# Two of a pair's four weight sums by a ScalarE copy and an accumulating DMA, their tile in the residual's slots

## The chip, the core and the metric

The kernel runs on one core of a Trainium2 chip. TensorE (PE, with its weight loads as PEld), VectorE (DVE), ScalarE (ACT), GpSimd (POOL) and SyncE (SP) each work through their own list of instructions in order; an instruction that waits for a semaphore holds back all that stand behind it on its engine. DMAs are issued here by SP and POOL (a few by ACT) and land later. The metric is the device time of one execution in microseconds.

## What is computed

One layer of a decoder trunk over 512 tokens of width 2048, all in f32: a gated linear attention (GLA) mixer, a squared-ReLU MLP, a gated projection of a per-layer embedding, and a final norm:

```python
u = rmsnorm(h, norm_mix[i])
h = h + gla_mixer(u, ...)                                            # projections, chunked scan, w_out
h = h + jnp.square(jax.nn.relu(rmsnorm(h, norm_mlp[i]) @ w_up[i])) @ w_down[i]   # 2048 -> 8192 -> 2048
gate = jax.nn.sigmoid(rmsnorm(h, norm_ple[i]) @ w_ple_gate[i])
h = h + gate * (p[i] @ w_ple_proj[i])
return rmsnorm(h, norm_final)
```

The change lies in the product with `w_up` alone.

## The kernel before

Activations lie transposed, features on the partitions and the 512 tokens in the free dimension. An f32 product is made of three matmuls on float32r operands: each operand is split into `hi` (a cast by ScalarE) and `lo` (value minus `hi`, by VectorE), and hi·hi, hi·lo and lo·hi are summed in PSUM.

**The MLP** takes most of the time. `up_group(g)`, g = 0 to 31, makes 256 of the 8192 hidden features. The product with `w_up` is done by the Strassen-Winograd scheme: of each pair of 128-row blocks (`kp`, 0 to 7) and the two 128-column halves, seven products on blocks of 128x128 by 128x256 take the place of eight. Beside the raw weight blocks B11, B12, B21, B22 it needs four sums of weights, T1 to T4. One step `k4` (0 to 3) of an up group covers two values of `kp`:

- SP loads `raw_up`, 128x4x256 (512 KB), into one of the 3 `raw` buffers, which it shares in turn with `raw_dn`.
- VectorE forms the sums in the tile `T` (128x2x4x128): at L780 two of them at once (B12 and B21, each plus B11), at L782 and L783 the other two, each from the one before.
- for each `kp` ScalarE casts the three raw blocks and the four sums into `whi_up` (L790, two instructions), VectorE subtracts into `wlo_up` (L791, two), and PE runs 21 matmuls (L797 to L799). `whi` and `wlo` have 4 buffers each, in turn for up and down.

After its four steps the up group's products are combined (tile `e`, by ScalarE L803 and VectorE L804 to L811), squared and split into `Sh` and `Sl` (L813 to L817).

`down_group(c, g)` adds 512 hidden features (two up groups) times `w_down` into 256 of the 2048 outputs: POOL loads the residual tile `h` from `h_d` in DRAM (L845), SP loads `raw_dn`, ScalarE and VectorE split it (`whi_dn` L130, `wlo_dn` L132), PE runs 24 matmuls, VectorE adds the product onto `h` (L854, two instructions, called the evacuation below), and POOL stores `h` to `h_d` (L860). In the last round (c = 15) `h` stays on chip in another tile.

The loop over `c` interleaves them. One up group with its share of down groups is called **a half** below: up steps 0 and 1, down, up step 2, down, up step 3, down, the combination, down. So a half has four T tiles, T_0 to T_3, and four h tiles, h_0 to h_3, in the order T_0, T_1, h_0, T_2, h_1, T_3, h_2, h_3. The two up groups of c = 0 have no down groups beside them; after the last up group eight down groups follow.

The buffers: `T` has one buffer of its own (`sum`); `h` takes one of the three buffers of the tag `ld` (`load`), which before the MLP hold the residual `xres` of the output projection. `sums` also gives the differences `D` of the activations before the MLP and the squares after it.

The order of each engine's list and the buffers that the tiles get are set when the program is built, by a scheduler that takes the instructions by the place where the code writes them and by a buffer becoming free; on the chip the lists are fixed, and semaphores let them wait for each other.

Of the kernel before, what the change touches and what calls it, by code (L numbers as in the profile page):

```python
# [9 lines left out]
F32 = mybir.dt.float32  # L10
# [4 lines left out]
ALU = mybir.AluOpType  # L15

P = 128
# [42 lines left out]
def trunk_kernel(ctx, tc, a, out):  # L60
    nc = tc.nc

    const = ctx.enter_context(tc.tile_pool(name="const", bufs=1))
    wpool = ctx.enter_context(tc.tile_pool(name="wpool", bufs=4))
# [9 lines left out]
    def slot(shape, name, dtype=F32):  # L74
        return spool.tile(shape, dtype, tag="s", name=name)
# [4 lines left out]
    def bank(name):  # L80
        return mm.tile([P, 512], F32, tag="mm", name=name)
# [53 lines left out]
    def w_rows(w, k0, nk, c0, nc_):  # L135
        return w[k0 * P:(k0 + nk) * P, c0:c0 + nc_].rearrange("(k p) c -> p k c", p=P)
# [89 lines left out]
    X = [None] * NK  # L226

    def load(shape, name):
        return wpool.tile(shape, F32, tag="ld", name=name, bufs=3)

    xc = [None] * (NK // 2)

    def x_load(cc):
        xc[cc] = load([P, NTT, 256], f"x_{cc}")
        nc.sync.dma_start(xc[cc], x2[:, cc * 256:(cc + 1) * 256].rearrange("(j p) c -> p j c", p=P))
# [69 lines left out]
    for k in range(NK):  # L305
# [6 lines left out]
        if k == 0:  # L312
# [5 lines left out]
            for b in range(2):  # L318
                t = slot([P, NK // 2, P], f"lr_w{b}", F32R)
# [264 lines left out]
    def load_gated(i):  # L584
        raw = load([P, T], f"gr_{i}")
        nc.gpsimd.dma_start(raw, gated_d[i])
        split_gated(i, raw)
# [68 lines left out]
    tpool = mlp.enter_context(tc.tile_pool(name="tpool", bufs=1))  # L656
# [8 lines left out]
    def wide(name):  # L665
        return tpool.tile([P, 8, HT], F32, tag="w", name=name)

    def sums(name):
        return tpool.tile([P, 2, 4, P], F32, tag="sum", name=name)

    acc2 = const.tile([P, T], F32, name="acc2")

# [31 lines left out]
    def operands(kp, u):  # L704

        a_, runs = operand_slots(kp)
        ub = u.rearrange("p k (h t) -> p (k h) t", h=2)
        d = sums(f"D_{kp}").rearrange("p a b c -> p (a b c)").rearrange("p (o t) -> p o t", t=HT)
        nc.vector.tensor_tensor(out=d[:, 0, :], in0=ub[:, 1, :], in1=ub[:, 3, :], op=ALU.subtract)
        nc.vector.tensor_tensor(out=d[:, 1, :], in0=ub[:, 0, :], in1=ub[:, 1, :], op=ALU.subtract)  # L710
        nc.vector.tensor_tensor(out=d[:, 2, :], in0=ub[:, 0, :], in1=d[:, 0, :], op=ALU.subtract)
        nc.vector.tensor_tensor(out=d[:, 3, :], in0=ub[:, 2, :], in1=d[:, 2, :], op=ALU.subtract)
        for n_run in range(len(runs[0])):
            o, n, hi = runs[0][n_run]
            lo = runs[1][n_run][2]
            for q_ in range(n):
                blk = (0, 2, 3)[o + q_]
                if q_ and (0, 2, 3)[o + q_ - 1] == blk - 1:
                    continue
                m = 2 if q_ + 1 < n and (0, 2, 3)[o + q_ + 1] == blk + 1 else 1  # L720
                src = ub[:, blk:blk + m, :]
                nc.scalar.copy(hi[:, q_:q_ + m, :], src)
                nc.vector.tensor_tensor(
                    out=lo[:, q_:q_ + m, :], in0=src, in1=hi[:, q_:q_ + m, :].bitcast(F32), op=ALU.subtract)
        nc.scalar.copy(a_[0], d)
        nc.vector.tensor_tensor(out=a_[1], in0=d, in1=a_[0].bitcast(F32), op=ALU.subtract)
# [4 lines left out]
    def evac_out(i, ps):  # L731
        kp = i // 2
        if i % 2 == 0:
            late["x"] = load([P, 2, T], f"xres_{kp}")
            nc.gpsimd.dma_start(late["x"], xT_d[i:i + 2].rearrange("k p t -> p k t"))
            if kp in (5, 6):
                late["u"] = extra([P, 2, T], f"u_{kp}")
            else:
                late["u"] = wide(f"u_{kp}").rearrange("p a t -> p (a t)").rearrange("p (a t) -> p a t", t=T)[:, 0:2, :]
            late[kp] = late["u"]  # L740
        h = late["x"][:, i % 2, :]
        nc.vector.tensor_tensor(out=h, in0=ps, in1=h, op=ALU.add)
        nc.vector.scalar_tensor_tensor(
            out=late["u"][:, i % 2, :], in0=h, scalar=vec("norm_mlp", i), in1=rb, op0=ALU.mult, op1=ALU.mult)
        add_squares(h, f"mlp_{i}", i == 0)
        if i % 2:
            nc.gpsimd.dma_start(h_d[i - 1:i + 1].rearrange("k p t -> p k t"), late["x"])
            if kp < 5:
                operands(kp, late["u"])
# [12 lines left out]
    w_up = a["w_up"].rearrange("o k c -> (o k) c")  # L762
# [9 lines left out]
    def up_group(g):  # L772

        ps = [bank(f"ps_up{g}_{b}").rearrange("p (a t) -> p a t", a=2) for b in range(4)]
        for k4 in range(NK // 4):
            raw = wpool.tile([P, 4, 256], F32, tag="raw", name=f"raw_up{g}_{k4}", bufs=3)
            nc.sync.dma_start(raw, w_rows(w_up, 4 * k4, 4, 256 * g, 256))
            rp = raw.rearrange("p (q k) (n c) -> p q (k n) c", q=2, n=2)
            t = sums(f"T{g}_{k4}")
            nc.vector.tensor_tensor(  # L780
                out=t[:, :, 0:2, :], in0=rp[:, :, 1:3, :], in1=rp[:, :, 0:1, :].broadcast_to([P, 2, 2, P]), op=ALU.add)
            nc.vector.tensor_tensor(out=t[:, :, 2, :], in0=t[:, :, 0, :], in1=rp[:, :, 2, :], op=ALU.add)  # L782
            nc.vector.tensor_tensor(out=t[:, :, 3, :], in0=t[:, :, 2, :], in1=rp[:, :, 3, :], op=ALU.add)  # L783
            for q_ in range(2):
                kp = 2 * k4 + q_
                hi = wpool.tile([P, 8, P], F32R, tag="whi", name=f"whi_up{g}_{kp}")
                lo = wpool.tile([P, 8, P], F32R, tag="wlo", name=f"wlo_up{g}_{kp}")
                for o, src in ((1, rp[:, q_, 1:4, :]), (4, t[:, q_, :, :])):
                    n = src.shape[1]
                    nc.scalar.copy(hi[:, o:o + n, :], src)  # L790
                    nc.vector.tensor_tensor(  # L791
                        out=lo[:, o:o + n, :], in0=src, in1=hi[:, o:o + n, :].bitcast(F32), op=ALU.subtract)
                for n, (xa, wb) in enumerate(PRODUCTS):
                    b, half = BANK[n]
                    xh, xl = OPS[kp][xa]
                    dst = ps[b][:, half, :]
                    nc.tensor.matmul(dst, lhsT=hi[:, wb, :], rhs=xh, start=kp == 0 and half == 0, stop=False)  # L797
                    nc.tensor.matmul(dst, lhsT=hi[:, wb, :], rhs=xl, start=False, stop=False)  # L798
                    nc.tensor.matmul(dst, lhsT=lo[:, wb, :], rhs=xh, start=False, stop=kp == NKP - 1 and (b == 3 or half == 1))  # L799
            yield  # L800

        e = wide(f"e_{g}")
        nc.scalar.copy(e[:, 4, :], ps[0][:, 0, :])  # L803
        nc.vector.tensor_tensor(out=e[:, 7, :], in0=ps[0][:, 1, :], in1=e[:, 4, :], op=ALU.subtract)  # L804
        nc.vector.tensor_tensor(out=e[:, 6, :], in0=e[:, 7, :], in1=ps[1][:, 0, :], op=ALU.subtract)
        nc.vector.tensor_tensor(
            out=e[:, 3:6:2, :], in0=ps[1][:, 1:2, :].broadcast_to([P, 2, HT]), in1=e[:, 6:8, :], op=ALU.add)
        nc.vector.tensor_tensor(out=e[:, 0:3:2, :], in0=ps[2], in1=e[:, 4:6, :], op=ALU.add)
        nc.vector.tensor_tensor(out=e[:, 1, :], in0=ps[3][:, 0, :], in1=e[:, 6, :], op=ALU.subtract)
        z = e[:, 0:4, :].rearrange("p (f h) t -> p f (h t)", f=2)  # L810
        nc.vector.scalar_tensor_tensor(  # L811
            out=z, in0=z, scalar=0.0, in1=r2.unsqueeze(1).broadcast_to([P, 2, T]), op0=ALU.max, op1=ALU.mult)
        nc.scalar.activation(out=z, in_=z, func=AF.Square)  # L813
        sh = slot([P, 2, T], f"Sh_{g}", F32R)
        sl = slot([P, 2, T], f"Sl_{g}", F32R)
        nc.scalar.copy(sh, z)
        nc.vector.tensor_tensor(out=sl, in0=z, in1=sh.bitcast(F32), op=ALU.subtract)  # L817
        S[g] = (sh, sl)
        yield
# [77 lines left out]
    for k in range(PLE // P):  # L897
# [3 lines left out]
        t = slot([P, 2, T], f"PT_{k}", F32R)  # L901
# [105 lines left out]
```

## Time and profile before

| | |
|---|---|
| time, median of 3 runs | 2396.48 us (2396.01 to 2397.42) |
| the profiled execution, time and span | 2396.97 us, 2395.1 us |
| PE busy | 2368.7 us (99%) |
| DVE, ACT, POOL busy | 1552.7 (65%), 869.2 (36%), 222.5 us (9%) |
| MLP, in the profile | from about 828 us to about 2130 us |

The profile is one execution taken by the hardware's profiler. A busy time counts an engine's own instructions, not DMA transfers; matmuls are pipelined, so that their durations overlap. A wait is put down to what released it. For a DMA the profile gives the time that its issue took on the queue's engine, and separately the time from its issue to its landing.

### The profile page before, as it was taken

To read this page: it belongs to the slowest core of one execution; us is meant where nothing else is said; L and a number is where in the kernel's file an instruction comes from. 1 tells how busy PE (TensorE), PEld (TensorE's weight loads), DVE (VectorE), ACT (ScalarE), POOL (GpSimd) and SP (SyncE) were. 2 spreads that over 40 slices of the span, in tenths; PEclk is the share of its full clock that TensorE was granted. 3 is DMA by queue.
4 is the path that set the end of the run, shared out by engine and by line. 5 is a ranking of instruction groups with operands and counts; after the bars stand their busy time and mean duration, and the time that the engine had idled before them with its cause. 6 is when DMAs were issued, how large, how long until landed. Compare 5 with 4: busy or idle time off the path is not lost.

```text
span 2395.1 us, 33417 instructions
## 1 busy us (share of the span) xinstructions
PE 2368.7 (99%) x13360; PEld 2079.5 (87%) x13360; DVE 1552.7 (65%) x2457; ACT 869.2 (36%) x1287; POOL 222.5 (9%) x326
## 2 busy tenths in 40 slices
PE   8999999999999899999999999999999999999998
PEld 6888888888888799999999999999999999988888
DVE  5664747447665687677676767767677776765344
ACT  5433324324333343333333333333333333343322
POOL 2000000000010001111111111111111111110000
PEclk9999999999999999999999999999999999999999
DMA  8323323232354345666666666666666666683222
GB/s 255 105 81 102 89 79 106 83 96 86 102 177 145 109 128 192 208 202 203 199 201 200 193 208 205 203 196 201 196 199 204 207 203 195 197 270 127 84 80 80
DMA packets 257804, 382.85 MB, mean 160 GB/s; under 512 B 14324, under 2 KB 203440, under 8 KB 257648
## 3 DMA queue, kind: packets, MB, share of 16 engines
q1 hardware_dynamic: 213344, 228.68, 30.8%
q0 software_dynamic: 42208, 151.89, 19.0%
q8 instruction: 105, 1.72, 0.3%
q10 hardware_dynamic: 2096, 0.14, 0.1%
q14 instruction: 51, 0.42, 0.1%
HBM read 302.02 MB, written 78.64 MB: 159 GB/s over the span
## 4 chain that ended last, share of the span: by engine, by line
PE 98%; DVE 1%; DMA 0%; issue 0%; ACT 0%; SPq 0%; ACTq 0%
PE ps_dn L140 10%; PE ps_dn L141 10%; PE ps_dn L142 10%; PE ps_up L799 9%; PE ps_up L797 9%; PE ps_up L798 9%; PE ps_g L142 2%; PE ps_v L140 2%; PE ps_g L140 2%; PE ps_g L141 2%; PE ps_wo L140 2%; PE ps_wo L141 2%; PE ps_og L140 2%; PE ps_og L142 2%; PE ps_og L141 2%; PE ps_v L142 2%
## 5 line engine op out<-in xcount | busy, mean ns | idle before, releaser
L140 PE MATMUL ps_dn<-Sh,whi_dn 128*128 128x512 f32 x1024 | 399.5, 390 | 0.0
L141 PE MATMUL ps_dn<-Sl,whi_dn 128*128 128x512 f32 x1024 | 399.4, 390 | 0.0
L142 PE MATMUL ps_dn<-Sh,wlo_dn 128*128 128x512 f32 x1024 | 398.3, 389 | 0.0
L797 PE MATMUL ps_up<-XS,whi_up 128*128 128x256 f32 x1024 | 290.5, 284 | 5.2 <-ACT whi_up L790 5.2
L790 ACT CAST whi_up<-raw_up 128x384 fp32r<-128x384 f32 x256 | 131.5, 514 | 443.7 <-PE ps_up L798 226.4
L799 PE MATMUL ps_up<-XS,wlo_up 128*128 128x256 f32 x1024 | 290.4, 284 | 0.0
L798 PE MATMUL ps_up<-XS,whi_up 128*128 128x256 f32 x1024 | 290.3, 283 | 0.0
L854 DVE TENSOR_TENSOR h<-h,ps_dn 128x512 f32<-128x512 f32 x256 | 172.1, 685 | 117.9 <-PE ps_dn L142 117.7
L130 ACT CAST whi_dn<-raw_dn 128x1024 fp32r<-128x1024 f32 x128 | 134.7, 1052 | 277.7 <-PE ps_dn L141 140.2
L142 PEld LDWEIGHTS ps_dn<-Sh,wlo_dn 128*128 128x128 f32 x1024 | 192.3, 188 | 40.7
L791 DVE TENSOR_TENSOR wlo_up<-raw_up,whi_up 128x384 fp32r<-128x384 f32 x256 | 142.0, 555 | 129.5 <-ACT whi_up L790 129.4
L140 PEld LDWEIGHTS ps_dn<-Sh,whi_dn 128*128 128x128 f32 x1024 | 192.6, 188 | 37.6
L141 PEld LDWEIGHTS ps_dn<-Sl,whi_dn 128*128 128x128 f32 x1024 | 192.6, 188 | 36.6
L799 PE MATMUL ps_up<-XA,wlo_up 128*128 128x256 f32 x768 | 218.3, 284 | 0.0
L798 PE MATMUL ps_up<-XA,whi_up 128*128 128x256 f32 x768 | 217.4, 283 | 0.0
L797 PE MATMUL ps_up<-XA,whi_up 128*128 128x256 f32 x768 | 217.0, 283 | 0.0
L797 PEld LDWEIGHTS ps_up<-XS,whi_up 128*128 128x128 f32 x1024 | 197.1, 192 | 5.8 <-ACT whi_up L790 5.3
L132 DVE TENSOR_TENSOR wlo_dn<-raw_dn,whi_dn 128x1024 fp32r<-128x1024 f32 x128 | 156.8, 1225 | 67.8 <-ACT whi_dn L130 65.4
L798 PEld LDWEIGHTS ps_up<-XS,whi_up 128*128 128x128 f32 x1024 | 197.2, 193 | 0.0
L799 PEld LDWEIGHTS ps_up<-XS,wlo_up 128*128 128x128 f32 x1024 | 197.1, 192 | 0.1
L791 DVE TENSOR_TENSOR wlo_up<-T,whi_up 128x512 fp32r<-128x512 f32 x256 | 176.1, 689 | 9.8 <-ACT whi_up L790 9.7
L790 ACT CAST whi_up<-T 128x512 fp32r<-128x512 f32 x256 | 157.1, 616 | 51.4 <-DVE T L783 51.4
(300 smaller groups left out, 4784.3 us busy)
## 6 DMA issues: line engine op xcount, KB each, us to landing
h<-h_d POOLq DMA_DIRECT2D x128, 512.0 KB, 4.3
raw_up<-in_w_up SPq DMA_DIRECT2D x128, 512.0 KB, 4.3
raw_dn<-in_w_down SPq DMA_DIRECT2D x128, 512.0 KB, 4.6
h_d<-h POOLq DMA_DIRECT2D x120, 512.0 KB, 3.5
raw_v<-in_gla_w_in SPq DMA_DIRECT2D x32, 512.0 KB, 3.8
raw_og<-in_gla_w_in SPq DMA_DIRECT2D x32, 512.0 KB, 3.8
raw_wo<-in_gla_w_out SPq DMA_DIRECT2D x32, 512.0 KB, 3.7
raw_wg<-in_w_ple_gate SPq DMA_DIRECT2D x32, 512.0 KB, 3.6
```

Of the source, the lines that this page charges most:

```text
L130: nc.scalar.copy(hi, raw)
L132: nc.vector.tensor_tensor(out=lo, in0=raw, in1=hi.bitcast(F32), op=ALU.subtract)
L140: nc.tensor.matmul(ps, lhsT=wa[0], rhs=wb[0], start=first, stop=False)
L141: nc.tensor.matmul(ps, lhsT=wa[0], rhs=wb[1], start=False, stop=False)
L142: nc.tensor.matmul(ps, lhsT=wa[1], rhs=wb[0], start=False, stop=last)
L790: nc.scalar.copy(hi[:, o:o + n, :], src)
L791: nc.vector.tensor_tensor(out=lo[:, o:o + n, :], in0=src, in1=hi[:, o:o + n, :].bitcast(F32), op=ALU.subtract)
L797: nc.tensor.matmul(dst, lhsT=hi[:, wb, :], rhs=xh, start=kp == 0 and half == 0, stop=False)
L798: nc.tensor.matmul(dst, lhsT=hi[:, wb, :], rhs=xl, start=False, stop=False)
L799: nc.tensor.matmul(dst, lhsT=lo[:, wb, :], rhs=xh, start=False, stop=kp == NKP - 1 and (b == 3 or half == 1))
L854: nc.vector.tensor_tensor(out=hs[:, i, :], in0=hs[:, i, :], in1=ps[i], op=ALU.add)
```

## The change

The first of the three VectorE additions on T is replaced. ScalarE copies the two raw blocks B12 and B21 of both values of `kp` into T (one instruction, 128x512). Then POOL issues two DMAs, one for each `kp`, that read the block B11 (128x128) once more from `w_up` in DRAM, twice through a source step of zero, and add it onto the two copies in SBUF (128x2x128, 128 KB each). The two remaining additions follow on VectorE as before.

T no longer has a buffer of its own: `sums` now takes its tile from the tag `ld`, which goes from 3 to 4 buffers, so the space is the same. What else calls `sums` moves with it.

```diff
     def load(shape, name):
-        return wpool.tile(shape, F32, tag="ld", name=name, bufs=3)
+        return wpool.tile(shape, F32, tag="ld", name=name, bufs=4)
...
     def sums(name):
-        return tpool.tile([P, 2, 4, P], F32, tag="sum", name=name)
+        return load([P, 2, 4, P], name)
...
             t = sums(f"T{g}_{k4}")
-            nc.vector.tensor_tensor(
-                out=t[:, :, 0:2, :], in0=rp[:, :, 1:3, :], in1=rp[:, :, 0:1, :].broadcast_to([P, 2, 2, P]), op=ALU.add)
+            nc.scalar.copy(t[:, :, 0:2, :], rp[:, :, 1:3, :])
+            for q_ in range(2):
+                r0 = (4 * k4 + 2 * q_) * P
+                nc.gpsimd.dma_start(
+                    t[:, q_, 0:2, :], w_up[r0:r0 + P, 256 * g:256 * g + P].unsqueeze(1).broadcast_to([P, 2, P]),
+                    accum_op=ALU.add)
             nc.vector.tensor_tensor(out=t[:, :, 2, :], in0=t[:, :, 0, :], in1=rp[:, :, 2, :], op=ALU.add)
             nc.vector.tensor_tensor(out=t[:, :, 3, :], in0=t[:, :, 2, :], in1=rp[:, :, 3, :], op=ALU.add)
```

Lines behind the first edit of `up_group` move down by four: L782 becomes L786, L783 becomes L787, L790 to L799 become L794 to L803, L845, L854 and L860 become L849, L858 and L864.

In the names below, `T8_1` is the tile of up group 8, step 1, and `h_2_6` the residual tile of round 2, down group 6; the number behind is only the tile's own. Up group 8 runs beside down groups 0 to 3 of round 3; the half ahead of it has `h_2_4` to `h_2_7`.

On VectorE, from the first sum of up group 8 to the last down group of the half ahead, before:

```order
L132 TENSOR_TENSOR wlo_dn2_6_8719<-raw_dn2_6_8715,whi_dn2_6_8717 128x1024
L780 TENSOR_TENSOR T8_0_8804<-raw_up8_0_8802 128x2x256
L782 TENSOR_TENSOR T8_0_8804<-T8_0_8804,raw_up8_0_8802 128x2x128
L783 TENSOR_TENSOR T8_0_8804<-T8_0_8804,raw_up8_0_8802 128x2x128
L854 TENSOR_TENSOR h_2_5_8616<-h_2_5_8616,ps_dn2_5_0_8614 128x512
L854 TENSOR_TENSOR h_2_5_8616<-h_2_5_8616,ps_dn2_5_1_8615 128x512
L132 TENSOR_TENSOR wlo_dn2_7_8769<-raw_dn2_7_8765,whi_dn2_7_8767 128x1024
```

and now:

```order
L132 TENSOR_TENSOR wlo_dn2_6_8783<-raw_dn2_6_8779,whi_dn2_6_8781 128x1024
L858 TENSOR_TENSOR h_2_5_8678<-h_2_5_8678,ps_dn2_5_0_8676 128x512
L786 TENSOR_TENSOR T8_0_8868<-T8_0_8868,raw_up8_0_8866 128x2x128
L858 TENSOR_TENSOR h_2_5_8678<-h_2_5_8678,ps_dn2_5_1_8677 128x512
L132 TENSOR_TENSOR wlo_dn2_7_8833<-raw_dn2_7_8829,whi_dn2_7_8831 128x1024
L787 TENSOR_TENSOR T8_0_8868<-T8_0_8868,raw_up8_0_8866 128x2x128
```

The first addition that reads T after the DMAs (L786) stands between the two halves of the evacuation of `h_2_5`, ahead of the second; in the same way L786 and L787 of T8_1 stand ahead of both halves of that of `h_2_6`, those of T8_2 ahead of `wlo_dn3_0`, and those of T8_3 ahead of the evacuation of `h_3_0`.

On ScalarE, around the third T of the same up group, before:

```order
L816 CAST Sh_7_8757<-e_7_8748 128x1024
L790 CAST whi_up8_3_8895<-raw_up8_1_8862 128x384
L790 CAST whi_up8_3_8895<-T8_1_8864 128x512
L130 CAST whi_dn3_0_8928<-raw_dn3_0_8926 128x1024
L790 CAST whi_up8_4_8965<-raw_up8_2_8959 128x384
```

and now:

```order
L820 CAST Sh_7_8821<-e_7_8812 128x1024
L780 COPY T8_2_9029<-raw_up8_2_9027 128x2x256
L794 CAST whi_up8_3_8963<-raw_up8_1_8928 128x384
L794 CAST whi_up8_3_8963<-T8_1_8930 128x512
L130 CAST whi_dn3_0_8996<-raw_dn3_0_8994 128x1024
```

The copy into T8_2 stands ahead of the casts of the fourth `kp` and of the first down group; it waits for its buffer, that is for the store of `h_2_6` to land.

On POOL, where the residual is loaded and stored, before:

```order
L860 DMA h_d_108<-h_2_5_8616 128x2x512
L845 DMA h_3_0_8924<-h_d_108 128x2x512
L860 DMA h_d_108<-h_2_6_8713 128x2x512
L845 DMA h_3_1_9021<-h_d_108 128x2x512
L860 DMA h_d_108<-h_2_7_8763 128x2x512
```

and now:

```order
L864 DMA h_d_108<-h_2_5_8678 128x2x512
L783 DMA T8_1_8930<-in_w_up 128x2x128 x2
L849 DMA h_3_0_8992<-h_d_108 128x2x512
L864 DMA h_d_108<-h_2_6_8777 128x2x512
L783 DMA T8_2_9029<-in_w_up 128x2x128 x2
L864 DMA h_d_108<-h_2_7_8827 128x2x512
L849 DMA h_3_1_9091<-h_d_108 128x2x512
```

Each pair of accumulating DMAs stands among the loads and stores of the residual. In the program built from the new code each T takes the buffer of the h with the same number in the half ahead (T8_1 that of `h_2_5`, T8_2 that of `h_2_6`), and each h that of the T of its own half (`h_3_0` that of T8_0).

## Rows read from the trace of the kernel before

**Rows 1.** The page's first part: busy us of each engine (share of the span) xinstructions.

```profile
PE 2368.7 (99%) x13360; PEld 2079.5 (87%) x13360; DVE 1552.7 (65%) x2457; ACT 869.2 (36%) x1287; POOL 222.5 (9%) x326
```

**Rows 2.** Busy time by stretch; last columns granted clock, DMA share, GB/s.

```profile
core 0: us, PE busy (x) PEld busy (x) DVE busy (x) ACT busy (x) POOL busy (x), PEclk, DMA share, GB/s
...
824.00:834.00 10.00, 5.31 (x16) 3.95 (x17) 9.11 (x28) 3.70 (x6) 0.40 (x1) 0.50 0.38 117
...
1000.00:2000.00 1000.00, 1000.00 (x6298) 909.52 (x6297) 716.70 (x1120) 355.64 (x548) 135.83 (x190) 1.00 0.63 201
```

**Rows 3.** What PE waited for, whole run: us in total, times, longest us.

```profile
PE ps_up L797 <- ACT whi_up L790: 5.2, 1, 5.2
PE ps_ts_mlp L206 <- DVE acc L679: 3.4, 1, 3.4
```

**Rows 4.** Groups by line, whole run: busy us, mean ns, idle before.

```profile
L854 DVE TENSOR_TENSOR h<-h,ps_dn 128x512 f32<-128x512 f32 x256 | 172.1, 685 | 117.9 <-PE ps_dn L142 117.7
...
L790 ACT CAST whi_up<-T 128x512 fp32r<-128x512 f32 x256 | 157.1, 616 | 51.4 <-DVE T L783 51.4
...
L780 DVE TENSOR_TENSOR T<-raw_up 128x512 f32<-128x512 f32 x128 | 88.6, 692 | 17.3 <-DMA raw_up<-in_w_up 13.2
...
L782 DVE TENSOR_TENSOR T<-T,raw_up 128x256 f32<-128x256 f32 x128 | 54.4, 425 | 4.2
L783 DVE TENSOR_TENSOR T<-T,raw_up 128x256 f32<-128x256 f32 x128 | 54.3, 424 | 3.2
```

**Rows 5.** ACT in order of time: start us, us, line; the same cast, one half apart.

```profile
1060.91 1.05 ACT L130 CAST whi_dn<-raw_dn 128x1024 fp32r<-128x1024 f32 x1 [1.47 <-issue]
...
1102.89 1.05 ACT L130 CAST whi_dn<-raw_dn 128x1024 fp32r<-128x1024 f32 x1 [1.47 <-issue]
```

**Rows 6.** DVE in order of time, in one half.

```profile
1064.77 0.69 DVE L780 TENSOR_TENSOR T<-raw_up 128x512 f32<-128x512 f32 x1 [1.55 <-DMA raw_up<-in_w_up]
...
1085.88 1.23 DVE L132 TENSOR_TENSOR wlo_dn<-raw_dn,whi_dn 128x1024 fp32r<-128x1024 f32 x1
...
1097.26 1.37 DVE L854 TENSOR_TENSOR h<-h,ps_dn 128x512 f32<-128x512 f32 x2 [2.56 <-PE ps_dn L142]
...
1100.93 0.56 DVE L791 TENSOR_TENSOR wlo_up<-raw_up,whi_up 128x384 fp32r<-128x384 f32 x1 [1.24 <-ACT whi_up L790]
1101.45 0.69 DVE L791 TENSOR_TENSOR wlo_up<-T,whi_up 128x512 fp32r<-128x512 f32 x1
```

**Rows 7.** POOL in order of time, in the same half.

```profile
1099.04 0.73 POOL L860 DMA_DIRECT2D h_d<-h  x1 [8.09 <-DVE h L854]
1102.66 0.71 POOL L845 DMA_DIRECT2D h<-h_d  x1 [2.90 <-DMA h_d<-h]
```

**Rows 8.** DMA issues, 1000 to 2000 us: queue, KB each, median us to landing.

```profile
raw_up<-in_w_up SPq DMA_DIRECT2D x96, 512.0 KB, 4.3
h_d<-h POOLq DMA_DIRECT2D x95, 512.0 KB, 3.5
h<-h_d POOLq DMA_DIRECT2D x95, 512.0 KB, 4.2
```

**Rows 9.** DMA issues of the whole run: POOL's 256 KB loads of the mixer.

```profile
gr<-gated_d POOLq DMA_DIRECT2D x12, 256.0 KB, 3.0
```

**Rows 10.** The tile h_d, 1060 to 1104 us: issue to landing of its loads and stores.

```profile
DMA to landing us min/median/max: 3.2/4.2/6.3
```

**Rows 11.** ACT in order of time where the MLP begins.

```profile
821.43 0.71 ACT L722 CAST XA<-u 128x256 fp32r<-128x256 f32 x2
824.04 1.04 ACT L725 CAST XS<-D 128x1024 fp32r<-128x1024 f32 x1 [1.91 <-DVE D L712]
828.02 1.14 ACT L790 CAST whi_up<-T 128x512 fp32r<-128x512 f32 x2 [2.93 <-DVE T L783]
```

**Rows 12.** DVE in order of time at the same place.

```profile
826.38 0.69 DVE L780 TENSOR_TENSOR T<-raw_up 128x512 f32<-128x512 f32 x1
```

## The prediction

> **What bounds the kernel now.** I read the engines' shares first, then busy time by stretch, then what PE waited for, and last one half of the MLP in order of time. PE is busy for 99% of the span [rows 1], and from 1000 to 2000 us for every microsecond, at the full granted clock [rows 2]. In the whole MLP PE waits once for ScalarE's cast of the first T and once for VectorE, 5.2 and 3.4 us, both where the MLP begins [rows 3]. VectorE is busy for 717 of those 1000 us, ScalarE for 356, POOL for 136 [rows 2], so work taken from VectorE is worth nothing by itself: the most that a faster way to T can win is the one wait of 5.2 us. A half lasts 42.0 us (the same cast stands at 1060.91 and 1102.89 [rows 5]), and it is set by PE. The question is therefore whether the new way to T still fits under 42.0 us.
>
> **What is removed, added and moved.** VectorE loses 128 additions of 0.692 us [rows 4], 88.6 us that lie beside PE. ScalarE gains 128 copies; the cast of the same shape takes 0.616 us [rows 4], together 79 us, on an engine that is idle two thirds of the time. POOL gains 256 issues; one of 256 rows, as these are, takes 0.72 us [rows 7], together 184 us, on an engine that is idle too. As busy time all this is covered. What counts is waiting, since each engine works in order.
>
> The new chain to a T is: copy 0.62, handing over to POOL 0.41 (the evacuation ends at 1097.26 + 1.37 = 1098.63 and POOL starts at 1099.04 [rows 6, 7]), the first DMA's issue 0.72, then the second DMA from its issue to its landing, which I call A. Before, all this was one VectorE instruction of 0.69. Taken alone the chain would be hidden, since T is formed long ahead of its use. But the new order ties each T to the one before it:
>
> - T_1 takes the buffer of h_1 of the half ahead. Its copy waits until that h is stored, the store waits for the second half of the evacuation, and that now stands on VectorE behind the first addition of T_0, which waits for T_0's DMAs. From T_0's landing to T_1's copy: 0.43 (L786) + 0.69 + 0.41 + 3.5 for the store [rows 4, 7, 8] = 5.0 us.
> - T_2 likewise: the evacuation of h_2 stands behind both additions of T_1. 0.85 + 1.37 + 0.41 + 3.5 [rows 4, 6, 8] = 6.1 us.
> - T_3 takes its weights from the raw buffer that `wlo_dn` of the half's first down group lets go, and this stands behind T_2's additions. 0.85 + 1.23 + 4.3 for the load [rows 4, 6, 8] = 6.4 us.
> - T_0 of the next half: its raw buffer is let go by the raw part of the last `wlo_up`, behind T_3's additions and the evacuation of h_0. 0.85 + 1.37 + (0.56 + 0.69 + 0.56) + 4.3 [rows 4, 6, 8] = 8.3 us; its other wait, for the store of h_0, is shorter (0.85 + 1.37 + 0.41 + 3.5 = 6.1).
>
> So there is a ring of four T's per half, in which PE does not occur: 25.8 us for these links, plus four times the chain itself, 4 x (0.62 + 0.41 + 0.72 + A) = 7.0 + 4A. **The ring takes 32.8 + 4A per half.** If this is less than 42.0 it is hidden by PE; above that, it sets the period, and PE waits. The point from which it decides is A = 2.3 us. The fourth buffer does not break the ring, since buffers are handed from h_k to T_k and back.
>
> What is A? The trace has no accumulating DMA. Below: loads by POOL take 4.2 us for 512 KB [rows 8] and 3.0 for 256 KB [rows 9]; carried on in a line, 128 KB take 2.4. Above: the longest landing of the residual in this half is 6.3 [rows 10]. Nearest is the load of h at 4.2: same queue, same stretch, the same 256 rows, one buffer in SBUF. An accumulating DMA moves fewer bytes, but reads its destination as well as its source, and the second one runs close behind the first; the destination's 128 KB would be 0.6 by the slope above, of which I add half, as the two reads can overlap. I take A = 4.5 and keep 2.4 and 6.3 as ends. With these the half takes 50.8 us (42.4 and 58.0).
>
> The ring runs from half 3, whose T_0 is the first to wait for a store of h in the loop, to half 31: 29 halves. 29 x (50.8 - 42.0) = 255 us. In the halves of c = 0 no h is stored and T has only its own chain; I cost them at nothing, since T has four buffers there and the four `whi` buffers let the casts run two up steps ahead of PE, which covers the chain of 0.62 + 0.41 + 0.72 + 4.5 = 6.3 us; without that cover their eight steps cost a chain each at most, 50 us, which I don't expect.
>
> Where the MLP begins T's sum stands late on VectorE, at 826.38 [rows 12], and PE waits for it. Now the copy can follow the casts of XA at 821.43 + 0.71 = 822.14 [rows 11]; the DMAs land at 822.14 + 0.62 + 0.41 + 0.72 + 4.5 = 828.4, and the two additions end at 829.2, where the cast of T started at 828.02 before [rows 11]. That is 1.2 us later for the first T; the second, issued 1.4 us behind, is then earlier than before. I cost this at nothing (ends: -5.2, the whole wait, and +3, with A = 6.3).
>
> **The sum** is made against the profiled execution, 2396.97 us (its span of 2395.1 and 1.9 around it), which is 0.5 above the median of the runs: 2397 + 255 = **2652 us**.
>
> **Rivals.**
> *The DMA is quick and the ring is hidden.* For it: the line through 3.0 and 4.2 us gives 2.4 for 128 KB, and then the ring takes 42.4. At A = 2.3 and below nothing changes: 2397 us. Against it: no row of a POOL transfer in the MLP is under 3.2 [rows 10], and these DMAs read two operands. The Trainium skill, page "DMA: Bandwidth & Descriptors", section "Anatomy of one DMA — SWDGE (gpsimd) path", has a fit for a plain transfer from GpSimd of about 2.0 us plus the bytes over 436e3, which makes 2.3 for 128 KB, and by it the ring would be just hidden, with 2397 us. By the same fit 256 and 512 KB would take 2.6 and 3.2, where this trace has 3.0 and 4.2 [rows 8, 9], so here the fit falls short. Chance 0.07.
> *Faster: the beginning of the MLP wins.* With A under 2.5 the first T lands (822.14 + 1.75 + A) before VectorE gets to 826.38, where its sum stood before [rows 11, 12]; 0.69 us of VectorE and up to the whole wait of 5.2 [rows 3] go, and with A under 2.3 nothing is lost later: 2392 us at best. Chance 0.03.
> *The accumulating DMA is much slower than any plain one*, because it reads, adds and writes back, or because its 256 rows of 512 B a piece crowd engines that are already 63% taken [rows 2]. Above A = 6.3 the half takes over 58.0: 2397 + 29 x 16.0 = 2861 us and more; A = 8 gives 64.8 and 3058 us. Chance 0.13.
> *PE's clock falls too.* Where the MLP begins, PE had only waits and little work, and from 824 to 834 us the clock granted was 0.50 of full [rows 2], the lower of its two levels (1.2 for 2.4 GHz). If every half brought this, PE would lose 5 us of its own work in 10: 47.0 in place of 42.0, still under the ring's 50.8, so it is mostly covered. It adds perhaps 2 us a half where PE's lateness reaches the evacuations, 60 us: 2710. It is inside the forecast's range, not beside it.
>
> **How the numbers follow.** The forecast (ring, A from 2.6 to 6.3) has a chance of 0.77; the same forecast with A between 2.4 and 2.6 lies within 30 us of no change and is counted in it. The rivals have 0.07, 0.03 and 0.13. The likeliest time is 2652. The range goes from 2440 (A = 2.7: 29 x 1.6 = 46) to 2900 (a little over A = 6.3, with DMAs 0.2 us slower in the four links, 23 us). About 0.10 is left out below (the hidden and the faster case) and 0.1 above. A difference of 0.2%, 5 us, is about what a measurement of this kernel can tell from no change: faster 0.03, within it 0.07, slower 0.90.
>
> **What would show it.** Right: halves of about 51 us between equal instructions; PE waiting in each half at the second up step and at the first down group, for `wlo_dn` and the casts of T; VectorE waiting at L786 for the accumulating DMA; ScalarE's copy waiting for the store of h; VectorE's busy time 89 us less and of no use. A is read from the DMA's issue and landing. Wrong: if PE stays at 1000 of 1000 us, the ring is hidden; if A is near 4.5 and the half still takes 42, then a link of the ring is not what I read from the order; if the half is longer than 32.8 + 4A, some other wait has joined in, PE's clock or slower loads first of all.

## The result, and the profile after

The time goes from 2396.95 us (median of 4 runs beside it) to **3098.83 us** (median of 4, 3094.62 to 3105.08): a ratio of 1.293, with a 95% interval of 1.291 to 1.295. The prediction was 2652 us with a range of 2440 to 2900: slower, as forecast, but by 702 us where 255 were forecast. The profiled execution took 3105.08 us, 3103.3 of them its span, so 708 more than the one before.

The page's first part and the row of POOL's DMA queue, to be set beside [rows 1]:

```profile
PE 2596.3 (84%) x13360; PEld 2235.2 (72%) x13360; DVE 1429.3 (46%) x2329; ACT 921.7 (30%) x1415; POOL 537.9 (17%) x582
...
q0 software_dynamic: 111840, 185.46, 23.6%
```

PE is idle for 16% of the span. No other engine is near full. A thousand microseconds of the MLP, in the columns of [rows 2]:

```profile
1300.00:2300.00 1000.00, 765.48 (x4047) 667.55 (x4046) 400.15 (x656) 252.11 (x412) 240.29 (x246) 0.85 0.54 146
```

Before, PE was busy there for 1000 of 1000 us at a clock of 1.00. Now it is busy for 765 at 0.85, a mean between the two levels of 1.2 and 2.4 GHz, and the DMA engines are less busy (0.54) than before (0.63), so they are not the bound either. What PE waits for in this stretch (us in total, times, longest); [rows 3] had one wait of 5.2 us and one of 3.4 in the whole run:

```profile
PE ps_dn L142 <- DVE wlo_dn L132: 174.1, 31, 7.2
PE ps_up L803 <- DVE wlo_up L795: 56.1, 15, 4.6
```

**One turn of the ring.** VectorE in order of time, from one T to the evacuation behind it:

```profile
1614.17 0.42 DVE L786 TENSOR_TENSOR T<-T,raw_up 128x256 f32<-128x256 f32 x1 [6.84 <-DMA T<-in_w_up]
1614.63 0.42 DVE L787 TENSOR_TENSOR T<-T,raw_up 128x256 f32<-128x256 f32 x1
1614.97 1.28 DVE L858 TENSOR_TENSOR h<-h,ps_dn 128x512 f32<-128x512 f32 x2
```

POOL in order of time:

```profile
1605.00 1.18 POOL L783 DMA_DIRECT2D T<-in_w_up  x1 [4.24 <-ACT T L780]
1610.56 1.21 POOL L783 DMA_DIRECT2D T<-in_w_up  x1 [4.38 <-issue]
1611.28 1.24 POOL L849 DMA_DIRECT2D h<-h_d  x1
1616.67 0.74 POOL L864 DMA_DIRECT2D h_d<-h  x1 [4.15 <-DVE h L858]
1621.08 1.24 POOL L783 DMA_DIRECT2D T<-in_w_up  x1 [3.67 <-ACT whi_up L794]
1626.38 1.21 POOL L783 DMA_DIRECT2D T<-in_w_up  x1 [4.07 <-issue]
```

ScalarE's copies:

```profile
1603.98 0.62 ACT L780 COPY T<-raw_up 128x512 f32<-128x512 f32 x1 [1.90 <-DMA h_d<-h]
...
1620.05 0.62 ACT L780 COPY T<-raw_up 128x512 f32<-128x512 f32 x1 [4.34 <-DMA h_d<-h]
```

Copy at 1603.98, first DMA at 1605.00, second at 1610.56, VectorE's first addition at 1614.17; then the second addition, the evacuation until 1616.25, the store at 1616.67, and with its landing the next copy at 1620.05. This is the ring of the prediction, member for member, and PE is not in it. The link from T to the next copy takes 5.88 us (6.1 were forecast). The way from copy to addition takes 10.19, and there 6.25 were forecast.

What ScalarE's copies waited for, and what VectorE waited for at its first addition, from 1300 to 2300 us:

```profile
ACT T L780 <- DMA raw_up<-in_w_up: 156.9, 31, 6.0
ACT T L780 <- DMA h_d<-h: 88.4, 30, 4.8
```

```profile
DVE T L786 <- DMA T<-in_w_up: 495.6, 62, 11.8
```

Between 1200 and 2200 us every copy into T_1 and T_2 is released by a store of h and every copy into T_3 and T_0 by a load of weights, as in the prediction's four links. In their order these take 5.4, 6.0, 7.3 and 8.9 us in the mean, where 5.0, 6.1, 6.4 and 8.3 were forecast.

The difference comes from the 4.38 us before the second DMA, which the profile puts down to "issue": POOL waits for nothing that the program asked for. When did the first DMA land? Looking at the stretches that hold only the issue at 1605.00 and only that at 1621.08 (last column: us from issue to landing):

```profile
T<-in_w_up POOLq DMA_DIRECT2D x1, 128.0 KB, 5.2
...
T<-in_w_up POOLq DMA_DIRECT2D x1, 128.0 KB, 5.0
```

1605.00 + 5.2 = 1610.2 and 1621.08 + 5.0 = 1626.1; the second DMAs start at 1610.56 and 1626.38, 0.3 to 0.4 us behind. In the next two pairs of the half the first DMA lands after 3.4 and 3.5 us, at 1642.45 and 1660.94, and the second starts at 1642.78 and 1661.28. In all 62 pairs between 1200 and 2200 us the second starts 0.32 us behind the landing of the first, after a wait of 2.3 to 5.6 us. **The second accumulating DMA is not issued before the first has landed.** Over the thousand microseconds, POOL's group (busy us, mean ns | idle before, and what ended it):

```profile
L783 POOL DMA_DIRECT2D T<-in_w_up x123 | 149.1, 1212 | 522.8 <-issue 215.7 <-ACT T L780 207.8 <-ACT whi_up L794 99.3
```

62 of these waits make 215.7 us. The same sight where the MLP begins, in the up groups without down groups, where no store of h is in the way:

```profile
850.78 1.21 POOL L783 DMA_DIRECT2D T<-in_w_up  x1 [2.58 <-issue]
854.66 1.20 POOL L783 DMA_DIRECT2D T<-in_w_up  x1 [2.67 <-issue]
858.64 1.21 POOL L783 DMA_DIRECT2D T<-in_w_up  x1 [2.78 <-issue]
862.46 1.20 POOL L783 DMA_DIRECT2D T<-in_w_up  x1 [2.61 <-issue]
```

One accumulating DMA every 3.9 us, eight to an up group: 31 us, and the up group takes 33 (from 865.8 to 898.8, VectorE's first additions of two groups), where it took 22.3 before.

### The profile page after: what moved, and what is told of

Read it like the earlier page. It is cut to its first block, busy times and chain, and to the rows that moved or that the text cites. A ratio compares the mean times of both kernels' runs of the same rounds, so it can differ in the third digit from the quotient of the medians.

```text
span 3103.3 us, 34182 instructions
## 1 busy us (share of the span) xinstructions
PE 2596.3 (84%) x13360; PEld 2235.2 (72%) x13360; DVE 1429.3 (46%) x2329; ACT 921.7 (30%) x1415; POOL 537.9 (17%) x582
## 3 DMA queue, kind: packets, MB, share of 16 engines
q0 software_dynamic: 111840, 185.46, 23.6%
## 5 line engine op out<-in xcount | busy, mean ns | idle before, releaser
L142 PE MATMUL ps_dn<-Sh,wlo_dn 128*128 128x512 f32 x1024 | 461.4, 451 | 327.5 <-DVE wlo_dn L132 327.5
L786 DVE TENSOR_TENSOR T<-T,raw_up 128x256 f32<-128x256 f32 x128 | 54.4, 425 | 987.5 <-DMA T<-in_w_up 958.2
L783 POOL DMA_DIRECT2D T<-in_w_up x256 | 310.3, 1212 | 1058.2 <-issue 450.2
L140 PE MATMUL ps_dn<-Sh,whi_dn 128*128 128x512 f32 x1024 | 448.4, 438 | 0.0
L141 PE MATMUL ps_dn<-Sl,whi_dn 128*128 128x512 f32 x1024 | 444.0, 434 | 0.0
L794 ACT CAST whi_up<-T 128x512 fp32r<-128x512 f32 x256 | 157.7, 617 | 924.7 <-DVE T L787 905.4
L803 PE MATMUL ps_up<-XA,wlo_up 128*128 128x256 f32 x768 | 237.1, 309 | 116.5 <-DVE wlo_up L795 115.9
L803 PE MATMUL ps_up<-XS,wlo_up 128*128 128x256 f32 x1024 | 309.6, 303 | 8.7 <-DVE wlo_up L795 8.4
L801 PE MATMUL ps_up<-XS,whi_up 128*128 128x256 f32 x1024 | 308.2, 301 | 8.8 <-ACT whi_up L794 8.8
L802 PE MATMUL ps_up<-XS,whi_up 128*128 128x256 f32 x1024 | 307.1, 300 | 0.0
L140 PEld LDWEIGHTS ps_dn<-Sh,whi_dn 128*128 128x128 f32 x1024 | 225.6, 220 | 45.7
L803 PEld LDWEIGHTS ps_up<-XA,wlo_up 128*128 128x128 f32 x768 | 159.5, 208 | 125.2 <-DVE wlo_up L795 124.7
L803 PEld LDWEIGHTS ps_up<-XS,wlo_up 128*128 128x128 f32 x1024 | 214.1, 209 | 13.2 <-DVE wlo_up L795 12.3
L801 PEld LDWEIGHTS ps_up<-XS,whi_up 128*128 128x128 f32 x1024 | 216.3, 211 | 9.4 <-ACT whi_up L794 8.9
L780 ACT COPY T<-raw_up 128x512 f32<-128x512 f32 x128 | 79.1, 619 | 483.0 <-DMA raw_up<-in_w_up 311.0
L802 PEld LDWEIGHTS ps_up<-XS,whi_up 128*128 128x128 f32 x1024 | 215.5, 210 | 0.0
```

The source lines that it names most:

```text
L140: nc.tensor.matmul(ps, lhsT=wa[0], rhs=wb[0], start=first, stop=False)
L141: nc.tensor.matmul(ps, lhsT=wa[0], rhs=wb[1], start=False, stop=False)
L142: nc.tensor.matmul(ps, lhsT=wa[1], rhs=wb[0], start=False, stop=last)
L780: nc.scalar.copy(t[:, :, 0:2, :], rp[:, :, 1:3, :])
L783: nc.gpsimd.dma_start(t[:, q_, 0:2, :], w_up[r0:r0 + P, 256 * g:256 * g + P].unsqueeze(1).broadcast_to([P, 2, P]), accum_op=ALU.add)
```

## Experiments

Two questions: what holds the second DMA, and is the rest of the way the ring that was predicted? The kernel's constructor sets aside 1024 bytes of each SBUF partition for the descriptors of POOL's DMAs (`dynamic_dma_scratch_size=1024` in `kernel`), in both kernels alike. Nothing of it was in the prediction.

**More space for descriptors.**

```diff
-    r2 = const.tile([P, T], F32, name="r2")
+    r2 = rb
...
-    nc = _bacc.Bacc("TRN2", ..., dynamic_dma_scratch_size=1024)
+    nc = _bacc.Bacc("TRN2", ..., dynamic_dma_scratch_size=3072)
```

> Edit: the SBUF set aside for the descriptors of POOL's DMAs goes from 1024 to 3072 bytes of a partition; to make room, r2 uses rb's tile (rb is read for the last time before r2 is written). In the trace of after the second accumulating DMA of a T is not issued 0.72 us behind the first but waits 2.5 to 4.4 us more, with no releaser shown. Theory 'space': the descriptors of two accumulating DMAs don't fit in 1024 bytes, so POOL waits for the first to drain. Then the wait of POOL at the accumulating DMA (215.7 us, 62 times in 1000 us) goes; a T takes 0.62 + 0.40 + 0.72 + 3.5 to 4.7 = 5.2 to 6.4 us from copy to landing in place of 9.5, a half 28.2 (the links as measured in after) + 21 to 26 = 49 to 54 us, and the time is 2600 to 2745 us. Theory 'one at a time': an accumulating DMA waits for the one before it whatever the space; then the waits stay and the time is 3099 +- 20. Theory 'crowding' (the wait comes from engines that are busy with other transfers): also 3099, within 50.

Measured: 2789.69 us, ratio 1.164 (1.162 to 1.166). POOL in order of time, what POOL waited for, and the DMAs of T (median us to landing), from 1200 to 2200 us:

```profile
1601.71 2.45 POOL L783 DMA_DIRECT2D T<-in_w_up  x2 [3.71 <-ACT whi_up L794]
1603.18 1.72 POOL L864 DMA_DIRECT2D h_d<-h  x1
```

```profile
POOL T L783 <- ACT T L780: 245.4, 36, 10.8
...
POOL T L783 <- ACT whi_up L794: 151.5, 37, 6.0
```

```profile
T<-in_w_up POOLq DMA_DIRECT2D x146, 128.0 KB, 5.2
```

Both DMAs now go out together ("x2"), the instruction behind them starts 1.47 us after the first, and the wait at "issue" is gone from the answer. 309 us of the 702 are back. "One at a time" and "crowding" fall: both wanted 3099. The time is 45 us above the end that "space" gave. That fits the second DMA's landing: with the first still under way beside it, it comes 5.3 us after the issue (median), where after, behind the first one's landing, it was 3.5 and the expectation allowed up to 4.7. The first DMA lands after 4.4 us in the mean in both kernels.

**Its control.** The same without the second edit (r2 in rb's tile, 1024 bytes).

> Control of the run with more space: only r2 moves to rb's tile, and the space for descriptors stays at 1024 bytes. All theories: 3099 us, within 0.5%, and the wait of POOL at the accumulating DMA as in after (about 216 us in 1000).

Measured: 3105.56 us, ratio 1.296 (1.293 to 1.298); POOL waits at "issue" for 214.0 us in 1000. The gain is the space's.

**Half of that space.** 1536 in place of 3072.

> As the run with 3072 bytes for descriptors (r2 in rb's tile), but with 1536. In the small space of 1024 plain DMAs of the same rows were not held, pairs of accumulating ones were. Theory 'two accumulating DMAs need a little more than 1024': no hold, 2790 us within 1%. Rival 'the space has to hold everything that is under way on POOL's queue, stores and loads of h too': holds of 1 to 3 us remain, 2850 to 3050 us.

Measured: 2822.37 us, ratio 1.178 (1.175 to 1.180), between the two. The accumulating DMAs of a T are no longer held, but the load of h behind them is, 30 times by up to 2.7 us:

```profile
POOL h L849 <- issue: 49.0, 30, 2.7
```

So the space has to hold what is under way on POOL's queue beside the pair as well, as the rival said, though the price, 33 us, is small. With 3072 bytes these waits are 4.7 us in 1000.

**Plain DMAs.** After, with 1024 bytes:

```diff
                 nc.gpsimd.dma_start(
-                    t[:, q_, 0:2, :], w_up[...].unsqueeze(1).broadcast_to([P, 2, P]),
-                    accum_op=ALU.add)
+                    t[:, q_, 0:2, :], w_up[...].unsqueeze(1).broadcast_to([P, 2, P]))
```

> After, with 1024 bytes for descriptors as there, but the two DMAs of a T are plain ones that overwrite instead of accumulating; so the addition in two of the four sums is left out, and nothing else. Same rows, same bytes written, the same waits in the program. Theory 'space, filled by what accumulating adds': the destination is not read, the descriptors fit, POOL's wait at the second DMA (216 us in 1000) goes, and the period is that of the run with more space or a little less: 28.2 + 4 x (0.62 + 0.40 + 0.72 + 3.5 to 5.6) = 49 to 58 us by the links of after, so 2600 to 2860 us; if the accumulation itself costs something beyond space, it is below the 2790 of the run with 3072 bytes. Rival 'the 256 rows of 512 bytes fill the space, accumulating or not': the wait stays, 3050 to 3110 us.

Measured: 2572.56 us, ratio 1.073 (1.071 to 1.075), 27 us below the expected span, since the four links between the T's take 26.3 us here, not the 28.2 of after that the expectation took. POOL isn't held at the pair; only the load of h behind it still waits, 23 us in 1000. The issue of a pair, the DMAs' landing, and the row of POOL's queue:

```profile
1607.66 1.43 POOL L783 DMA_DIRECT2D T<-in_w_up  x2 [8.64 <-ACT T L780]
```

```profile
T<-in_w_up POOLq DMA_DIRECT2D x166, 128.0 KB, 2.7
```

```profile
q0 software_dynamic: 54496, 185.46, 22.3%
```

It is the accumulation that fills the space, not the 256 rows. And the accumulation costs time of its own: 2.7 us to landing for the plain ones, two at a time, against 5.2 with 3072 bytes (medians of both DMAs of a pair), and 217 us between the two kernels. The queue's row tells what it adds: the plain kernel has 54496 packets on POOL's queue, the accumulating ones 111840, that is 224 more for each of the 256 DMAs, with the same bytes.

**One accumulating DMA for each T.**

```diff
-            nc.scalar.copy(t[:, :, 0:2, :], rp[:, :, 1:3, :])
-            for q_ in range(2): ...two accumulating DMAs
+            nc.scalar.copy(t[:, 0, 0:2, :], rp[:, 0, 1:3, :])
+            ...one accumulating DMA, into t[:, 0, 0:2, :]
+            nc.vector.tensor_tensor(out=t[:, 1, 0:2, :], in0=rp[:, 1, 1:3, :], in1=rp[:, 1, 0:1, :].broadcast_to([P, 2, P]), op=ALU.add)
```

> After, but only the first pair of blocks of a T goes by copy and accumulating DMA; the sums of the second pair are formed by VectorE as before. Half of the accumulating DMAs go, and none has another one close ahead of it. Theory 'ring, with space for one': no wait of POOL within a T; a T takes 0.4 (copy of half the size) + 0.40 + 3.5 to 5.5 (issue to landing), and VectorE's half sum of 0.43 lies beside it; a half takes 26 to 28 + 4 x (4.3 to 6.3) = 43 to 53 us, 2430 to 2720 us. Theory 'each accumulating DMA costs a fixed sum on the DMA engines': half of the 702 us, so 2740 to 2760.

Measured: 2543.16 us, ratio 1.061 (1.059 to 1.063). Half of the accumulating DMAs cost 147 us, not half of 702: the price lies in the pair. Part of this is that PE hides the first 42.0 us of a half: the ring of 46.7 stands 4.7 us over it, that of 65.1 stands 23.1 over it.

**Only the sharing of slots.** VectorE forms all sums as before; `sums` and the four buffers as in after.

> One part of the change alone: T takes its buffer among the four of the residual, but VectorE forms all four sums as before, without copy and DMA. Theory 'ring' (T waits for T through the stores and VectorE's order, and what makes it too long is the way from copy to landing): the ring is 28.2 + 4 x 0.69 = 31 us a half, under PE's 42.0, so the time is that of before, 2397 us within 0.2%. Rival 'the sharing of slots costs': well above, up to 3099 less the DMAs' part; 2500 or more.

Measured: 2424.82 us, ratio 1.012 (1.011 to 1.014). Neither as expected nor the rival: the ring is hidden, but 28 us are lost. In the profiled execution (2415.9 us) a half takes 42.74 us against 41.98. VectorE waits for the weights of T, and PE a little for VectorE (1200 to 2200 us):

```profile
DVE T L780 <- DMA raw_up<-in_w_up: 220.5, 43, 6.3
...
PE ps_up L799 <- DVE wlo_up L791: 7.3, 13, 1.8
```

T is formed with little to spare, which before was so only where the MLP begins. PE's waits of 7.3 us are but a part of the loss. Of the 19 us between the two profiled spans (2414.1 and 2395.1), PE is idle for 11 more and busy for 8 more (2376.4 us); what causes them, I leave open.

**Only copy and DMAs.** T in its own single buffer as before, the residual in three.

> The other part alone: copy and accumulating DMAs as in after, but T keeps its own single buffer and the residual its three. Theory 'ring, with the DMAs as the long member': the old ring is gone, but with one buffer T's copy waits until the T before has been read; a T then takes 9.5 us (copy to landing as in after) + 0.85 (two additions) + about 3.5 (casts and subtractions of both halves of T) = 14 us, a half 55 to 60 us, and this holds in all 32 halves: 2810 to 2970 us. Rival 'the sharing of slots costs': 2397 to 2450 us.

Measured: 3051.81 us, ratio 1.273 (1.270 to 1.276); a half takes 62.4 us, some 2 more than the upper end. So the DMAs are slow without the sharing of slots too. What the sharing costs beside them this run doesn't tell, since the single buffer makes a ring of its own: the copies into T_2 and T_3 wait for the last subtraction from the T before.

**T in two own buffers**, 3072 bytes, the order of after. The pool `spool2` lies unused behind the start of the MLP.

```diff
-            t = sums(f"T{g}_{k4}")
+            t = extra([P, 2, 4, P], f"T{g}_{k4}")
```

> After with 3072 bytes for descriptors, and T no longer among the residual's buffers but in two of its own (the 8 KB that only the start of the MLP uses). The order of the work is that of after. Theory 'ring': the links over the stores of h are gone; what is left is the chain over the raw buffers, three T's a half (T0 to T2, T2 to T3, T3 to the next T0): 3 x 7.3 (copy to landing, as with 3072 bytes) + 8 + 8 + 9 = 47 us a half: 2500 to 2600 us, against 2790 with the shared buffers. Rival 'the transfers themselves are too slow in the crowd': 2790, as before.

Measured: 2616.26 us, ratio 1.092 (1.089 to 1.094), 16 us over the expected span. ScalarE's copy no longer waits for a store of h, but for the weights:

```profile
ACT T L780 <- DMA raw_up<-in_w_up: 238.5, 72, 6.9
```

With the links over the stores taken out, 173 us of the 393 that were left come back. The DMAs are the same in number and shape, but land sooner (4.0 us in the median, against 5.2).

**A step ahead: two misses, and two more.** The load, the copy and the DMAs of a T were written one up step ahead of its additions, first with after's buffers.

```diff
+        ahead = form(0)          # raw_up, copy, the two DMAs
+        yield
...
+            rp, t = ahead
+            if k4 + 1 < NK // 4:
+                ahead = form(k4 + 1)
```

> After with the load of raw_up, the copy and the two accumulating DMAs of a T written one up step earlier (for the first T of a group before the last evacuation of the group ahead), so that VectorE's additions to T come a step after its DMAs. Nothing else moves; 1024 bytes for descriptors. Theory 'ring': a store of h no longer waits for a T whose DMAs have just been issued; the way from copy to landing, 8.5 to 10.2 us, lies beside PE's step of 10.5 us; 2400 to 2520 us, with the hold of POOL at the second DMA still there, but hidden. Rival 'PE, DMA engines or POOL are overrun by 256 more transfers': 2750 us or more, whatever the order.

Measured: 3076.12 us, ratio 1.283 (1.281 to 1.285).

> The same, and 3072 bytes for descriptors (r2 in rb's tile). Theory 'ring': T is there 4 us earlier still, and POOL isn't held: 2395 to 2440 us; not under 2390, since PE is busy nearly throughout before and only the 5.2 us wait at the start of the MLP can be won. The sharing of slots alone cost 28 us (2425), which may or may not come back with T formed earlier. Rival as in the run without the space: 2600 us or more.

Measured: 2750.63 us, ratio 1.148 (1.146 to 1.150). Both far above what I expected, so I gave T and the weights buffers of their own (T in `extra`, `raw` 4, `ld` 3):

> A step ahead once more, now with buffers to be ahead in: T in two of its own, four raw buffers, three for the residual, 3072 bytes for descriptors. The run a step ahead without these changed little, since raw_up of a T to come took its buffer from the weights of a down group behind the T at hand. Theory 'ring': no T waits for the T just before it; a T waits for the last reader of the T two before, 7.3 + 0.85 + about 3 us, that is 10 to 11.5 us a step, beside PE's 10.5: 2400 to 2520 us. Rival 'crowd': above 2700.

Measured: 2715.67 us, ratio 1.133 (1.131 to 1.135).

> The same with three own buffers for T, but with the space for descriptors left at 1024 (the third buffer takes the room). Theory 'ring': POOL is still held 2.5 to 4.4 us at every second accumulating DMA, but a T is begun more than a step ahead of its use, so that 9.5 us from copy to landing lie beside PE's step: 2400 to 2500 us. If instead the hold counts by itself (POOL's queue of loads and stores of h behind it): 2600 to 3000.

Measured: 2922.32 us, ratio 1.220 (1.218 to 1.222).

Missed again; with two own buffers the kernel written ahead is even 99 us slower than the one that isn't. VectorE and POOL, in order of time, with two own buffers and 3072 bytes:

```profile
1652.58 0.42 DVE L794 TENSOR_TENSOR T<-T,raw_up 128x256 f32<-128x256 f32 x1 [8.98 <-DMA T<-in_w_up]
1652.92 0.68 DVE L866 TENSOR_TENSOR h<-h,ps_dn 128x512 f32<-128x512 f32 x1
```

```profile
1647.71 2.44 POOL L782 DMA_DIRECT2D T<-in_w_up  x2 [2.83 <-ACT T L779]
```

VectorE still stands for 9 us at the first addition to T, and starts it 4.9 us after the DMAs' issue: not a step behind them, but right behind. Its list of instructions shows why (up group 12, with the rows between left out):

```
L794 TENSOR_TENSOR T12_1_10525<-T12_1_10525,raw_up12_1_10523 128x2x128
...
L795 TENSOR_TENSOR T12_1_10525<-T12_1_10525,raw_up12_1_10523 128x2x128
L803 TENSOR_TENSOR wlo_up12_0_10532<-raw_up12_0_10463,whi_up12_0_10531 128x384
```

The code writes the additions to T_1 a step after the subtractions of T_0; the scheduler put them ahead. The trace agrees: in up groups 3 to 30 both additions to T_1 run before both subtractions from T_0 itself (`wlo_up<-T`), in the kernels with two and with three own buffers. So the wait moved with the DMAs, and T_1's lateness now also holds what T_0 still has to give. I changed where the code stands and took that for the order on the engine, without reading the order. In the first two of these four kernels, with after's buffers, the additions to T_1 stay behind those subtractions; there ScalarE's copies wait for loads of weights, 246 and 236 us in 1000.

That this is the whole reason for the misses was read, not tested. All four times lie where the rivals had them ("overrun by 256 more transfers", "crowd", "the hold counts by itself"). Against overrun DMA engines speaks their busy share between 1200 and 2200 us: 0.56, 0.67, 0.66 and 0.61 in the four, no more than the 0.70 of the faster kernel with two own buffers. That the hold counts by itself, in the kernel with three own buffers and 1024 bytes, was not tested.

## Why the prediction was wrong, and where it was right

**The ring was right.** In each kernel with the four buffers and after's order I took the mean way from ScalarE's copy to VectorE's first addition (61 to 86 of them between 1200 and 2200 us) and the mean distance of these additions, times four:

| kernel | copy to addition | half by the prediction's links, 25.8 + 4 x that | half measured |
|---|---|---|---|
| after | 9.37 us | 63.3 us | 65.1 us |
| 3072 bytes | 7.33 us | 55.1 us | 55.4 us |
| 1536 bytes | 7.39 us | 55.4 us | 56.0 us |
| plain DMAs | 5.46 us | 47.6 us | 48.0 us |
| one accumulating DMA | 4.51 us | 43.8 us | 46.7 us |

The links taken from the trace of before hold within 2 us in all but the last, where VectorE's own half sum, 4 x 0.43 us, comes on top.

**The step that failed is the chain to a T**, "copy 0.62, handing over to POOL 0.41, the first DMA's issue 0.72, then the second DMA". It has the second DMA leave 0.72 us behind the first. In fact it left 3.7 to 5.6 us behind in the half shown, when the first had landed, and 4.7 in the mean between 1200 and 2200 us: 4.0 us a T that were counted at nothing, 16 a half. A was not what made it longer: I took 4.5, and in the half shown the second DMAs landed after 3.4 to 4.5 us, 3.5 in the mean of 62. That A was a us too long hid 4 of the 16. With copy and handover (1.02) and the mean of the four first DMAs (4.28), the pause (0.34) and the mean of the four second ones (3.7) the chain is 9.3; I had 6.25. Four times the 3.1 us that were missing are 12.5 of the 14.3 us by which a half of 65.1 exceeds the predicted 50.8. The nearest rows told of 256 rows a DMA and of its landing, but before has no accumulating DMA, so no row of it could show the hold; the setting of 1024 bytes stood in the code.

With the space the predicted sum is nearly met: the measured chain of 7.33 makes A = 7.33 - 1.75 = 5.6, and 32.8 + 4 x 5.6 = 55.2 against 55.4; 2790 us lies inside the range, though with A 1.1 us above the 4.5 that I took for likeliest.

**The halves without h were no free ride.** I costed the halves up to the first with a store of h at nothing, because T has four buffers there, and named 50 us without that cover. Between VectorE's first additions of up group 0 and up group 3 lie 116.8 us, before 69.1: 47.7 lost. The cover was for a wait that each T has once; but with 1024 bytes POOL issues one accumulating DMA at a time, every 3.9 us, and that is a rate, which no number of buffers hides. That the loss is near the 50 us is chance: those were eight chains one after the other, with no hold in them. With 3072 bytes the same stretch loses 18.5.

**The sum of the profiled executions:** 4.1 us until the first addition (831.2 against 827.1; the prediction had 1.2 and counted none), 47.7 until up group 3, 28 halves of 65.16 in place of 41.98, that is 649.0, 19.4 more in the last up group, and 12.1 less behind it: 708.

**The rivals.** *Hidden* and *faster* are out. The Trainium skill's fit (page "DMA: Bandwidth & Descriptors", section "Anatomy of one DMA — SWDGE (gpsimd) path"), from which 2.3 us was the estimate for 128 KB, came nearest where it belongs: plain DMAs landed after 2.7. It says nothing of accumulating ones. *Much slower than any plain one* gave 3058 us at A = 8, near the time, but not by its reason: a single accumulating DMA landed after 3.5 us (the median, with one for each T); two in a row took 8. *PE's clock falls* came true: PE's busy time grew by 228 us over the same matmuls, at a granted clock of 0.85 in the loop. It costs little where the ring sets the pace, since the measured halves lie 0.3 to 1.8 us above the ring's in four of the five kernels.

**What would show it.** VectorE waiting at L786, the copy waiting for the store of h, PE waiting at `wlo_dn`: all there. Halves of 51 us, as between the two casts of [rows 5]: 65. VectorE's busy time 89 us less: 123, but 56 of them went as well where only the slots were shared and its instructions were the same (1496.6 us busy), so these 56 are not the additions'; that leaves 67 of the 89, and I have no reason for the difference. I wrote that a half longer than 32.8 + 4A means "some other wait has joined in, PE's clock or slower loads first of all"; a wait had joined in, but a third one, on POOL's own queue.

## What to carry to other kernels

Before a step goes from an engine to a DMA, ask what the DMA's queue holds at a time, not only how long one DMA takes: two that don't fit run one after the other, and "issue" in front of a DMA instruction, ending just when the one before lands, is how that looks. A DMA that stands in the place of an instruction of 0.7 us puts its whole latency into every ring of buffers that it touches, so follow these rings from buffer to buffer, in the lists of the engines and not in the code, before trusting idle engines. And work that was shared in time by a wide margin, as T's sum was, is not idle work to be moved at will: PE was busy for 99% and VectorE was not, and there was nothing to win.

## What the runs showed of the hardware

- POOL holds the issue of a DMA while the space for its queue's descriptors is taken: with 1024 bytes two accumulating DMAs of 256 rows don't go out together, with 1536 they do, and two plain ones do with 1024. The Trainium skill, page "Debugging Trainium Hangs", section "4. Descriptor Overflow", names too many descriptors for that space as a cause of a hang; here it was a silent wait of 2.3 to 5.6 us in each of 62 pairs, and no hang.
- Accumulating 128 KB onto SBUF from DRAM in 256 rows takes 3.5 us to landing (medians of the second of a pair with 1024 bytes, and of the only one in the kernel with one for each T). Where a pair goes out together, the first lands after 4.3 us and the second after 5.3 with 3072 bytes, and plain ones of the same shape after 2.6 and 3.9 (medians). The first of a pair isn't faster when it is held apart: with 1024 bytes it takes 3.5 us in T_0 and T_3 and 5.0 to 5.4 in T_1 and T_2, and what makes that difference was not tested.
- An accumulating DMA puts 224 packets more on the queue than the plain one, for the same bytes.
